# Where the LayerNorm and sum work between out-projection and FFN stands: order, rings and placement

## The chip, the cores and the metric

The kernel runs on one core of a Trainium2 chip. The metric is device time of one launch in microseconds. Three runs of the kernel before took 2832.81, 2822.79 and 2829.03 us, so the median is 2829.03 us.

## The reference

One layer of a streaming encoder over 17 chunks of 128 tokens (2048 new frames and 8 running streams of 16), all in float32, model width 1024, FFN width 4096:

```python
h = W_out [ gMLP heads (u * (W_s v + b)) || Mamba-2 SSD heads ] (x W_in)
x = LayerNorm(ALPHA * x + h)                      # "LN1", its result is called x1
x = LayerNorm(ALPHA * x + relu(x W1)^2 W2)        # "LN2", the output y
```

LayerNorm subtracts the mean over the 1024 features, multiplies by rsqrt(variance + 1e-5) and a gain, and adds a bias. ALPHA is 2^0.25.

## The kernel before, in words

The program has four stages: the mixer's heads, the out-projection with LN1, the first FFN product (FFN1) and the second (FFN2) with LN2. Matmuls are float32 in three passes: `split` rounds an operand to a high part (a cast on ACT, line 55) and leaves a low part (a subtraction on DVE, line 56), and the products hi·hi, hi·lo and lo·hi are summed in PSUM. So an operand is usable in full only after ACT and then DVE have touched it.

**Out-projection** (lines 617 to 712). The 17 chunks stand in 16 groups: the first is chunks 0 and 1, the last is 15 and 16, the rest one chunk each. A chunk takes 96 matmuls of 128x512 (16 slices of the 2048 mixed features, three passes, two halves of the output). The weights `wout` are held in eight tiles. Ahead of a group its mixed heads are loaded as `mxs` (gMLP part) and `mys` (SSD part, through a transpose to `myt`) into the shared ring `stage` (called `sp` in the functions) and split into `mx`. After a group, the chunk of x is loaded into `xr`, two scalar_tensor_tensor add the PSUM banks to it (line 708), `layer_norm` (lines 603 to 613) writes the result to another tile `x1`, and that is stored to DRAM.

**Sums for the FFN** (`Sums`, lines 728 to 790). FFN1 multiplies blocks of 2x2 with seven products in place of eight (Strassen's scheme in Winograd's form). It needs sums of token blocks of x1 and sums of w1 blocks. `x_piece(b, j)` loads two chunks of x1 (`xts`, four DMAs each), transposes them to `xtt` (line 43), makes four sums on DVE (lines 761 to 767) and stores seven parts to DRAM `xv`; `w1_piece` does the like for the weights (`w1p`). The pieces of token block 0 and the w1 sums are made during the out-projection (`during_out_proj`); those of blocks 1 and 2 are written in the FFN's steps g = 3, 6 and 9 of the block before. In the kernel before, the tiles `xts`, `xtt` and `xsum` all come from the ring `stage`.

**FFN1** (lines 793 to 910): 48 steps, 3 token blocks by 16 weight groups, each of seven products in the order 1, 6, 2, 7, 5, 4, 3. A product takes 12 matmuls of 128x384 (128x320 in block 2) from an x operand `xt` (from `xr`, loaded out of `xv`) and a weight operand `w` (from `w1l`, `w1r` or the sums `w1s`). The weights of a step are split during the step before, into a ring of ten tiles.

**FFN2** (lines 912 to 1080) makes seven products too, and `finish` does LN2 of a chunk. At the end of the program only `finish` of chunks 12 and 13 remains: statistics on DVE, rsqrt and the scaled mean `fnm` on POOL (lines 76, 77, 1000), the normalisation on ACT (line 1002), the gain and the bias on DVE (lines 1003, 1004), and the store.

**What sets the order.** The source gives the work in program order, and a scheduler with an estimate of the engines' times writes the order of each engine's queue ahead of the run; on the chip each engine takes its queue strictly in turn. What may go early is held back only by data and by the rings. All DMAs of these stages are issued by one queue, SP's, also strictly in turn: a DMA that waits for its data holds back all that stand behind it. An `x_piece` that is written in a late step, but whose x1 is long in DRAM and whose ring has room, can be put far ahead of that step.

## Time and profile before

| | us |
|---|---|
| median of three runs | 2829.03 |
| the profiled execution, its own time | 2822.72 |
| its span | 2821.0 |
| out-projection: first to last matmul | 1068.3 to 1467.9 |
| FFN1: first matmul to the stage's steady state | 1474.7 to about 1560 |
| FFN1 to its end | about 2159 |
| FFN2: last matmul | about 2807 |
| tail without matmuls | 2807 to 2821.0 |

TensorE (PE) is busy for 98% of the span, VectorE (DVE) for 64%, ScalarE (ACT) for 39% and GpSimd (POOL) for 14%. The mean granted clock is 0.99 of full speed. Idle time of PE is therefore rare and stands in a few places, which the profile's windows and PE's timeline show. In a timeline row, the bracket behind an instruction tells how long its engine had been idle before it and what released it. The rows that carry the argument are shown in the prediction.

### The profile page before, as it was taken

Reading aid. Unit: us, or ns where it says so; the run is one execution under the profiler, and the core shown is the slowest. Engines: PE = TensorE matmul, PEld = TensorE weight load, DVE = VectorE, ACT = ScalarE, POOL = GpSimd, SP = SyncE. Lnnn points to the kernel's source line nnn. Section 1 sums busy time; section 2 is a strip of 40 time slices with the busy share of each in tenths; the row PEclk is TensorE's granted clock in tenths of the full one; section 3 lists DMA queues with packets and bytes.
Section 4 is the critical chain, followed back from the end, with each engine's and each line's share of the span. In section 5 each row is a group of like instructions: output and inputs, shape, how many; then the busy total and the mean of one; then the engine's idle time right before and its main releaser. Section 6 shows DMA issues by size and latency. Waiting matters only on the chain.

```text
span 2821.0 us, 42133 instructions
## 1 busy us (share of the span) xinstructions
PE 2753.9 (98%) x15814; PEld 2525.6 (90%) x15814; DVE 1816.1 (64%) x2836; ACT 1096.0 (39%) x2024; POOL 395.1 (14%) x547
## 2 busy tenths in 40 slices
PE   9999999999999998999989999999999999999998
PEld 8988899999999997887879999999999888888886
DVE  6766667645585457665558667667775356644887
ACT  5445423323333333100115556556665323333343
POOL 2214223323233312000100000000000000000022
PEclk9999999999999999999999999999999999999999
DMA  9897888766697768888579858667877468855764
GB/s 316 257 297 250 281 288 272 228 221 217 218 305 220 244 218 302 279 260 273 159 217 342 292 214 286 222 223 259 276 233 259 152 233 300 299 173 190 272 206 171
DMA packets 492316, 699.83 MB, mean 248 GB/s; under 512 B 74560, under 2 KB 379088, under 8 KB 485584
## 3 DMA queue, kind: packets, MB, share of 16 engines
q1 hardware_dynamic: 492112, 697.14, 74.8%
q8 instruction: 124, 2.03, 0.3%
q14 instruction: 80, 0.66, 0.1%
HBM read 474.04 MB, written 223.00 MB: 247 GB/s over the span
## 4 chain that ended last, share of the span: by engine, by line
PE 77%; DMA 12%; DVE 6%; issue 1%; ACT 1%; POOL 1%; SPq 1%; DVEq 0%; ACTq 0%; POOLq 0%
PE pf L858 22%; PE pf L1075 22%; PE psfl L231 13%; PE pstl L239 10%; PE po L683 4%; PE yd L446 2%; DMA w1p<-in_w_ff 2%; DMA w1s<-w1p 2%; PE pf L1040 2%; DMA v<-v 1%; DMA xv<-xtt 1%; PE st L483 1%; DMA v<-vo 1%; DMA e<-at 1%; PE yo L489 1%
## 5 line engine op out<-in xcount | busy, mean ns | idle before, releaser
L858 PE MATMUL pf<-xt,w 128*128 128x384 f32 (+1 forms) x4032 | 671.8, 329 | 14.6 <-ACT w L55 11.4
L858 PEld LDWEIGHTS pf<-xt,w 128*128 128x128 f32 x4032 | 669.2, 189 | 17.4 <-ACT w L55 12.3
L1075 PE MATMUL pf<-w,ht 128*128 128x512 f32 x2688 | 618.2, 389 | 0.0
L1075 PEld LDWEIGHTS pf<-w,ht 128*128 128x128 f32 x2688 | 504.6, 188 | 104.6
L231 PE MATMUL psfl<-xw,w 128*128 128x384 f32 (+1 forms) x2880 | 494.9, 330 | 0.0
L231 PEld LDWEIGHTS psfl<-xw,w 128*128 128x128 f32 x2880 | 475.5, 188 | 9.0 <-issue 8.6
L239 PE MATMUL pstl<-w,xw 128*128 128x256 f32 (+1 forms) x3264 | 411.0, 286 | 8.4 <-ACT w L55 6.5
L239 PEld LDWEIGHTS pstl<-w,xw 128*128 128x128 f32 x3264 | 396.4, 190 | 21.0 <-issue 11.8
L683 PE MATMUL po<-wout,mx 128*128 128x512 f32 x1632 | 379.5, 394 | 12.0 <-ACT mx L55 8.1
L683 PEld LDWEIGHTS po<-wout,mx 128*128 128x128 f32 x1632 | 309.2, 190 | 79.1 <-ACT mx L55 8.8
L56 DVE TENSOR_TENSOR ht<-hr,ht 128x1536 fp32r<-128x1536 f32 (+1 forms) x84 | 132.3, 1577 | 128.0 <-ACT ht L55 126.5
L76 POOL TENSOR_SCALAR frs<-fmv 128x1 f32<-128x1 f32 x17 | 8.9, 524 | 1291.6 <-DVE fmv L996 1291.0
L55 ACT CAST ht<-hr 128x1536 fp32r<-128x1536 f32 (+1 forms) x84 | 112.2, 1337 | 194.7 <-PE pf L1075 142.0
L56 DVE TENSOR_TENSOR w<-w1s,w 128x512 fp32r<-128x512 f32 x192 | 132.0, 691 | 41.0 <-ACT w L55 36.0
L55 ACT CAST w<-w1s 128x512 fp32r<-128x512 f32 x192 | 118.3, 619 | 64.1 <-PE pf L858 57.0
L308 DVE SCALAR_TENSOR_TENSOR acc<-raw,cw,acc 128x640 f32<-128x640 f32 (+1 forms) x108 | 111.4, 1031 | 14.1 <-ACT acc L302 12.7
L56 DVE TENSOR_TENSOR w<-w2r,w 128x512 fp32r<-128x512 f32 x144 | 93.8, 686 | 36.8 <-ACT w L55 36.6
L55 ACT CAST w<-w2r 128x512 fp32r<-128x512 f32 x144 | 83.3, 618 | 87.3 <-PE pf L1075 56.9
L438 ACT ACTIVATE e<-e,nacum 128x128 f32<-128x128 f32 x272 | 83.6, 389 | 66.8 <-POOL e L69 66.7
L55 ACT CAST w<-w1r 128x512 fp32r<-128x512 f32 x96 | 59.4, 618 | 98.6 <-PE pf L858 95.3
L247 ACT ACTIVATE gt<-gt 128x256 f32<-128x256 f32 (+1 forms) x116 | 52.3, 451 | 95.9 <-DVE gt L246 95.9
L849 ACT ACTIVATE hc<-hc 128x384 f32<-128x384 f32 (+3 forms) x144 | 87.1, 608 | 1.8
(214 smaller groups left out, 2875.4 us busy)
## 6 DMA issues: line engine op xcount, KB each, us to landing
w1s<-w1s SPq DMA_DIRECT2D x48, 1024.0 KB, 6.7
hr<-hv SPq DMA_DIRECT2D x56, 768.0 KB, 6.1
w2r<-in_w_ff SPq DMA_DIRECT2D x112, 256.0 KB, 5.6
w<-w_x SPq DMA_DIRECT2D x12, 2048.0 KB, 10.5
w1r<-in_w_ff SPq DMA_DIRECT2D x48, 512.0 KB, 6.7
hv<-hs SPq DMA_DIRECT2D x32, 768.0 KB, 5.2
ws<-in_w_in SPq DMA_DIRECT2D x34, 512.0 KB, 7.7
e<-at SPq DMA_DIRECT2D x34, 512.0 KB, 6.7
```

The source lines that it names most:

```text
L55: nc.scalar.copy(hi, src)
L56: nc.vector.tensor_sub(lo, src, hi.bitcast(F32))
L231: nc.tensor.matmul(ps[:, :n], w[:, a, k, f * P:(f + 1) * P], xw[:, b, k, o:o + n], start=(q, i, k) == KORDER[0], stop=(q, i, k) == KORDER[-1])
L239: nc.tensor.matmul(ps[:, :n], xw[:, a, k, j * P:(j + 1) * P], w[:, b, k, :n], start=(q, i, k) == KORDER[0], stop=(q, i, k) == KORDER[-1])
L308: nc.vector.scalar_tensor_tensor(aa, raw[:, k:k + npr], cw[:, ft, k:k + 1], aa, op0=ALU.mult, op1=ALU.add)
L438: nc.scalar.activation(e[:, h], e[:, h], AF.Exp, bias=s["nacum"][:, i:i + 1])
L446: nc.tensor.matmul(yd[:, h * HD:(h + 1) * HD], e[:, h], xdt[:, h * HD:(h + 1) * HD], start=True, stop=True)
L683: nc.tensor.matmul(acc[c][d], m[c][k // 4][:, a, k % 4], W[q][:, w, i, d * 512:(d + 1) * 512], start=k == 0 and (a, w) == (0, 0), stop=k = ...
L849: nc.scalar.activation(t, t, AF.Square)
L858: nc.tensor.matmul(o, W[i][:, u, k], X[i][:, v, k, :n], start=q + k == 0 and not more, stop=q == 2 and k == 3, skip_group_check=True)
L1040: nc.tensor.matmul(ps[d], h[:, u, k, f], w[d][:, v], start=k + f + q == 0, stop=(k, f, q) == (n - 1, 1, 2))
L1075: nc.tensor.matmul(acc[l], h[:, u, m, j * P:(j + 1) * P], w[m][:, v], start=kg + q + m == 0, stop=(kg, q, m) == (3, 2, 3))
```

## The change

Five edits.

1. The tiles of `x_piece` come from a ring that the caller gives. During the out-projection it is a new ring `xp` of three tiles; in the FFN it is still `stage`, and a small copy on GpSimd from the current step's `c11` into the tile `xts` stands ahead of its loads, so that a piece written at step g cannot start before that step's product 2 is done.
2. LN1 of chunks 15 and 16 is not done in the out-projection. The residual sum is stored as `x0`, and `late_norm` loads it again at FFN1 steps (0, 11) and (0, 13), with the gain and the bias, normalises and stores x1.
3. LN1 works in place in `xr`; the second tile `x1` is gone.
4. In the FFN the ring `wr` (raw weights) is allocated first on the left side, and `x4` first on the right side ahead of `ho`, so that they lie over other tiles of the out-projection than before.
5. `finish` of chunks 12 and 13, the last two, normalises on DVE alone: four half-width scalar_tensor_tensor per chunk in place of one ACT and two DVE instructions, and a store for each half.

```diff
@@ mixer program
+    x0_d = {c: dr.tile([P, D], F32, name=f"x0_{c}") for c in range(NCH - LATE, NCH)}
...
-    out_proj(tc, right, psA, tail, A, dr, small, stage, rsqrt, split, yg_d, ys_d, x1_d, sums.during_out_proj)
-    ffn(tc, psA, A, O, dr, small, stage, rsqrt, split, x1_d, sums)
+    out_proj(tc, right, psA, tail, A, dr, small, stage, rsqrt, split, yg_d, ys_d, x0_d, x1_d, sums.during_out_proj)
+    ffn(tc, psA, A, O, dr, small, stage, rsqrt, split, x0_d, x1_d, sums)
@@ out_proj
             tp = rpool("to", 2)
+            xring = rpool("xp", 3)
...
-            o = tp.tile([P, D], F32, name="x1", tag="x1")
-            layer_norm(nc, small, rsqrt, o, x, g, b)
-            nc.sync.dma_start(x1_d[c], o)
-        done(n, ring)
+            if c < NCH - LATE:
+                layer_norm(nc, small, rsqrt, x, x, g, b)
+            nc.sync.dma_start(x1_d[c] if c < NCH - LATE else x0_d[c], x)
+        done(n, ring, xring)
@@ Sums
+LATE = 2
...
-    def tokens(self, c):
-        s = self.sp.tile([P, 4, 256], F32, name="xts", tag="st")
+    def tokens(self, c, ring, after):
+        s = ring.tile([P, 4, 256], F32, name="xts", tag="st")
+        if after is not None:
+
+            self.nc.gpsimd.tensor_copy(s[:, 0, :1], after)
         load_blocks(self.nc, s, self.x1_d[c])
-        t = self.sp.tile([P, KD, P], F32, name="xtt", tag="st")
+        t = ring.tile([P, KD, P], F32, name="xtt", tag="st")
         flip(self.nc, t, s)
         return t
...
-        s = self.sp.tile([P, 2, 4, P], F32, name="xsum", tag="st")[:, :, :, :m]
+        s = ring.tile([P, 2, 4, P], F32, name="xsum", tag="st")[:, :, :, :m]
...
-            self.x_piece(0, n // 2 - 2)
+            self.x_piece(0, n // 2 - 2, xring)
@@ ffn
+    wr = pool("wr", 3)
     rawp = pool("raw", 2)
     wp = pool("w4", 10)
     xp = pool("x3", 3)
-    wr = pool("wr", 3)
+    xp4 = pool("x4", 4, first, side="right")
     hop = pool("ho", 2, first, side="right")
-    xp4 = pool("x4", 4, first, side="right")
     sump = pool("ws", 2, first, side="right")
...
+    seen = [None]
...
             ahead(i)
+        seen[0] = c11[:, :1]
...
+    def late_norm(c):
+        t, g1, b1 = (sp.tile([P, D], F32, name=f"ln{i}", tag="st") for i in range(3))
+        nc.gpsimd.tensor_copy(t[:, :1], seen[0])
+        nc.sync.dma_start(t, x0_d[c])
+        nc.sync.dma_start(g1, A["ln1_g"].unsqueeze(0).to_broadcast([P, D]))
+        nc.sync.dma_start(b1, A["ln1_b"].unsqueeze(0).to_broadcast([P, D]))
+        layer_norm(nc, small, rsqrt, t, t, g1, b1)
+        nc.sync.dma_start(x1_d[c], t)
...
         if b < 2 and g in (3, 6, 9):
-            sums.x_piece(b + 1, g // 3 - 1)
+            sums.x_piece(b + 1, g // 3 - 1, sp, seen[0])
+        if b == 0 and g in (11, 13):
+            late_norm(NCH - LATE + (g - 11) // 2)
...
         rsqrt(rs, mv[:, 1:2], 1.0, EPS)
+        if c in THIRDS[2][0]:
+
+            o = sp.tile([P, D], F32, name="yo", tag="st")
+            halves = [slice(512 * d, 512 * d + 512) for d in range(2)]
+            for h in halves:
+                nc.vector.scalar_tensor_tensor(o[:, h], y[c][:, h], mv[:, 0:1], g2[:, h], op0=ALU.subtract, op1=ALU.mult)
+            for h in halves:
+                nc.vector.scalar_tensor_tensor(o[:, h], o[:, h], rs, b2[:, h], op0=ALU.mult, op1=ALU.add)
+                nc.sync.dma_start(O["y"][c][:, h], o[:, h])
+            return
         nm = small.tile([P, 1], F32, name="fnm")

```

How the engines' queues move, at three places. First, DVE where the first group of the out-projection (chunks 0 and 1) ends. `mx` from `mxs` is chunk 2's gMLP part, `po` are the first group's PSUM banks. Before:

```order
L777 TENSOR_TENSOR w1p_12433<-w1p_12432,w1p_12433 128x4x128
L778 TENSOR_TENSOR w1p_12432<-w1p_12432 128x4x128
L779 TENSOR_TENSOR w1p_12432<-w1p_12433,w1p_12432 128x4x128
L56 TENSOR_TENSOR mx_12075<-mxs_12073,mx_12075 128x512
L780 TENSOR_TENSOR w1p_12433<-w1p_12433,w1p_12432 128x4x128
L56 TENSOR_TENSOR mx_12078<-mxs_12073,mx_12078 128x512
L43 STREAM_TRANSPOSE myt_12086<-mys_12081 128x4x8x32
L56 TENSOR_TENSOR mx_12088<-myt_12086,mx_12088 128x512
L56 TENSOR_TENSOR mx_12091<-myt_12086,mx_12091 128x512
L708 SCALAR_TENSOR_TENSOR xr_12110<-xr_12110,po_11682 128x512
```

And in the changed kernel:

```order
L785 TENSOR_TENSOR w1p_12434<-w1p_12433,w1p_12434 128x4x128
L786 TENSOR_TENSOR w1p_12433<-w1p_12433 128x4x128
L711 SCALAR_TENSOR_TENSOR xr_12115<-xr_12115,po_11684 128x512
L711 SCALAR_TENSOR_TENSOR xr_12115<-xr_12115,po_11685 128x512
L787 TENSOR_TENSOR w1p_12433<-w1p_12434,w1p_12433 128x4x128
L609 BN_STATS lst_12121<-xr_12115 128x6
L711 SCALAR_TENSOR_TENSOR xr_12117<-xr_12117,po_11686 128x512
L609 BN_STATS lst_12121<-xr_12115 128x6
L711 SCALAR_TENSOR_TENSOR xr_12117<-xr_12117,po_11687 128x512
L788 TENSOR_TENSOR w1p_12434<-w1p_12434,w1p_12433 128x4x128
L609 BN_STATS lst_12134<-xr_12117 128x6
L56 TENSOR_TENSOR mx_12077<-mxs_12075,mx_12077 128x512
```

The four residual sums of chunks 0 and 1 and three of their statistics, which stood behind chunk 2's splits, now stand ahead of the first of them.

Second, SP's queue around the loads of FFN1's first step (`w1l`, `w1r`, `w1s` are its weights, `xr` from `xv0` its token sums, the others are stores of x1 sums and of LN1). Before, behind 40 DMAs on pieces of block 1 that stand between the store of chunk 13's x1 and this place:

```order
L819 DMA xr_14447<-xv0_11517 128x1536
L827 DMA w1l_14425<-in_w_ff1 128x4x128
L829 DMA w1r_14427<-in_w_ff1 128x1024
L819 DMA xr_14455<-xv0_11517 128x1536
L827 DMA w1l_14487<-in_w_ff1 128x4x128
L760 DMA xv1_11518<-xtt_15921 128x4x128
L763 DMA xv1_11518<-xsum_15923 128x4x128
L764 DMA xv1_11518<-xsum_15923 128x4x128
L766 DMA xv1_11518<-xtt_15921 128x4x128
L831 DMA w1s_14429<-w1s0_11520 128x2048
L831 DMA w1s_14491<-w1s1_11521 128x2048
L819 DMA xr_14463<-xv0_11517 128x1536
```

And in the changed kernel, where no DMA of block 1's pieces stands here any more:

```order
L706 DMA xr_14342<-in_x 128x1024
L836 DMA w1l_14394<-in_w_ff1 128x4x128
L838 DMA w1r_14396<-in_w_ff1 128x1024
L714 DMA x1_14_124<-xr_14131 128x1024
L836 DMA w1l_14456<-in_w_ff1 128x4x128
L706 DMA xr_14344<-in_x 128x1024
L828 DMA xr_14400<-xv0_11519 128x1536
L828 DMA xr_14408<-xv0_11519 128x1536
L838 DMA w1r_14458<-in_w_ff1 128x1024
L828 DMA xr_14416<-xv0_11519 128x1536
L714 DMA x0_15_127<-xr_14342 128x1024
L840 DMA w1s_14398<-w1s0_11522 128x2048
```

The first weights stand right behind the load of chunk 15's x, and `w1s` stands behind the store of `x0_15`.

Third, DVE at the end of the program. Before:

```order
L1024 TENSOR_TENSOR y15_21298<-y15_21298,pf_24766 128x512
L56 TENSOR_TENSOR w2_25365<-w2r_25363,w2_25365 128x512
L996 BN_AGGR fmv_25273<-st11_21331 128x2
L56 TENSOR_TENSOR w2_25368<-w2r_25363,w2_25368 128x512
L970 BN_STATS st14_21334<-y14_21297 128x6
L56 TENSOR_TENSOR w2_25379<-w2r_25377,w2_25379 128x512
L56 TENSOR_TENSOR w2_25382<-w2r_25377,w2_25382 128x512
L970 BN_STATS st15_21335<-y15_21298 128x6
```

And in the changed kernel:

```order
L56 TENSOR_TENSOR w2_25384<-w2r_25379,w2_25384 128x512
L991 BN_STATS st14_21350<-y14_21313 128x6
L56 TENSOR_TENSOR w2_25395<-w2r_25393,w2_25395 128x512
L56 TENSOR_TENSOR w2_25398<-w2r_25393,w2_25398 128x512
L991 BN_STATS st15_21351<-y15_21314 128x6
L56 TENSOR_TENSOR ht_25457<-hr_25455,ht_25457 128x1536
L1034 TENSOR_TENSOR yo_25244<-yo_25244,g2_21316 128x1024
L1017 BN_AGGR fmv_25320<-st14_21350 128x2
L1034 TENSOR_TENSOR yo_25270<-yo_25270,g2_21316 128x1024
```

The four full-width products and sums behind the ACT instruction have become eight half-width ones behind the statistics.

More of the change, by code (lines that the diff above doesn't have):

```diff
@@ L616, in out_proj @@
 @with_exitstack
-def out_proj(ctx, tc, right, ps, tail, A, dr, small, sp, rsqrt, split, yg_d, ys_d, x1_d, done):
+def out_proj(ctx, tc, right, ps, tail, A, dr, small, sp, rsqrt, split, yg_d, ys_d, x0_d, x1_d, done):
     nc = tc.nc
@@ L738, in __init__, with x_piece @@
         self.w1 = [dr.tile([P, 2, 1024], F32, name=f"w1s{g}") for g in range(NG)]
-    def tokens(self, c):
-        s = self.sp.tile([P, 4, 256], F32, name="xts", tag="st")
+    def tokens(self, c, ring, after):
+        s = ring.tile([P, 4, 256], F32, name="xts", tag="st")
+        if after is not None:
+            self.nc.gpsimd.tensor_copy(s[:, 0, :1], after)
         load_blocks(self.nc, s, self.x1_d[c])
-        t = self.sp.tile([P, KD, P], F32, name="xtt", tag="st")
+        t = ring.tile([P, KD, P], F32, name="xtt", tag="st")
         flip(self.nc, t, s)
         return t
-    def x_piece(self, b, j):
+    def x_piece(self, b, j, ring, after=None):
         nc = self.nc
         if j < len(THIRDS[b][0]):
-            l, r, m = self.tokens(THIRDS[b][0][j]), self.tokens(THIRDS[b][1][j]), P
+            l, r, m = *(self.tokens(THIRDS[b][i][j], ring, after) for i in range(2)), P
         else:
-            t = self.tokens(ODD)
+            t = self.tokens(ODD, ring, after)
             m = P // 2
@@ L782, in w1_piece, with during_out_proj @@
             nc.sync.dma_start(self.w1[g][:, k], w[k].rearrange("p k f n -> p (k f n)"))
-    def during_out_proj(self, n, ring):
+    def during_out_proj(self, n, ring, xring):
         for g in range(NG * n // 13, min(NG * (n + 1) // 13, NG)):
@@ L788, in during_out_proj, with ffn @@
         if n in (4, 6, 8):
-            self.x_piece(0, n // 2 - 2)
+            self.x_piece(0, n // 2 - 2, xring)
 @with_exitstack
-def ffn(ctx, tc, ps1, A, O, dr, small, sp, rsqrt, split, x1_d, sums):
+def ffn(ctx, tc, ps1, A, O, dr, small, sp, rsqrt, split, x0_d, x1_d, sums):
     nc = tc.nc
```

## The prediction

> **What bounds the kernel now.** I read the page's chain of waits first, then PE's timeline for its gaps, then windows around each gap, then the other engines' rows inside it.
>
> ```profile
> PE 77%; DMA 12%; DVE 6%; issue 1%; ACT 1%; POOL 1%; SPq 1%; DVEq 0%; ACTq 0%; POOLq 0%
> 1750.00:1820.00 70.00, 70.00 (x405) 70.00 (x404) 46.83 (x81) 38.61 (x70) 0.00 (x0) 1.00 0.65 233
> 2737.00:2807.00 70.00, 70.00 (x310) 57.71 (x308) 56.65 (x71) 29.58 (x37) 15.44 (x21) 1.00 0.61 214
> ```
>
> The columns of a window are its length, the busy time (and count) of PE, PEld, DVE, ACT and POOL, the granted clock, the DMA share and GB/s. PE leads the chain, and the two windows, in FFN1 and FFN2, have PE busy in all of their 70 us. There nothing but fewer matmuls could gain, and the change removes none; the first also gives FFN1's pace, 70/405 = 0.1728 us per matmul. What can be won stands in PE's gaps:
>
> ```profile
> 1101.13 7.49 PE L683 MATMUL po<-wout,mx 128*128 128x512 f32 x24 [0.37 <-ACT wout L636]
> 1115.64 3.02 PE L683 MATMUL po<-wout,mx 128*128 128x512 f32 x12 [1.55 <-DVE wout L637]
> 1124.94 203.43 PE L683 MATMUL po<-wout,mx 128*128 128x512 f32 x896 [1.55 <-DVE wout L637]
> ...
> 1334.50 133.39 PE L683 MATMUL po<-wout,mx 128*128 128x512 f32 x576 [6.13 <-ACT mx L55]
> 1474.66 4.71 PE L858 MATMUL pf<-xt,w 128*128 128x384 f32 x12 [6.76 <-ACT w L55]
> 1483.99 17.69 PE L858 MATMUL pf<-xt,w 128*128 128x384 f32 x84 [4.62 <-ACT w L55]
> 1503.87 56.43 PE L858 MATMUL pf<-xt,w 128*128 128x384 f32 x315 [2.19 <-ACT hc L861]
> ```
>
> Two gaps lie in reach of the change: 6.13 us at 1328 to 1334 in the out-projection, and the passage to FFN1, which idles 6.76 + 4.62 + 2.19 = 13.6 us. A gap costs more than itself, since the clock falls behind it:
>
> ```profile
> 1334.50 5.73 PE L683 MATMUL po<-wout,mx 128*128 128x512 f32 x13 [6.13 <-ACT mx L55]
> 1330.00:1340.00 10.00, 5.50 (x13) 4.34 (x14) 8.93 (x14) 2.28 (x4) 2.13 (x2) 0.66 0.87 267
> 1470.00:1480.00 10.00, 4.58 (x12) 3.56 (x12) 9.97 (x15) 3.46 (x3) 0.93 (x1) 0.65 1.07 368
> 1480.00:1490.00 10.00, 6.01 (x19) 6.01 (x20) 9.13 (x14) 5.74 (x9) 1.94 (x4) 0.50 1.03 377
> 1500.00:1510.00 10.00, 7.81 (x37) 7.49 (x36) 7.88 (x14) 4.76 (x9) 0.00 (x0) 0.83 1.07 343
> ```
>
> With a granted clock of 0.66, 13 matmuls took 5.73 us. The steady rate is (133.39 - 2.8)/576 = 0.2267 us, so 13 should take 2.95: 2.8 us lost.
>
> **The change, part by part.** The sum is made against the profiled execution, 2822.72 us, which is 6.3 below the median of the runs shown (2829.03). A difference under 0.3%, some 8.5 us, cannot be told from none here.
>
> *A: the passage (edits 1, 2, 4).* The rows inside it:
>
> ```profile
> 1459.54 3.68 SPq L37 DMA_DIRECT2D xts<-x  x8
> 1468.12 0.39 SPq L827 DMA_DIRECT2D w1l<-in_w_ff  x1
> ...
> 1472.62 1.47 ACT L55 CAST xt<-xr 128x1536 fp32r<-128x1536 f32 x1 [14.08 <-DMA xr<-xv]
> ...
> 1476.76 1.09 SPq L831 DMA_DIRECT2D w1s<-w1s  x2
> 1480.06 4.60 SPq L37 DMA_DIRECT2D xts<-x  x4
> 1483.32 0.62 ACT L55 CAST w<-w1s 128x512 fp32r<-128x512 f32 x1 [5.10 <-DMA w1s<-w1s]
> ```
>
> From the last out-projection matmul (1334.50 + 133.39 = 1467.9) to the end of the third PE row (1560.3), 411 matmuls take 92.4 us. At the pace above they need 71.0, so 21.4 are lost: 13.6 idle, the rest a slow clock. The cause is SP's order: loads and stores of block 1's and 2's pieces (`xts`, `xv`) stand ahead of `w1l` (issued 1468.12) and `w1s` (1476.76), whose cast could begin only at 1483.32. Edit 1 takes these pieces away from here, and edits 2 and 4 take the LN1 work and let the weights' ring lie over tiles that fall free early. I place what is left of the waits from the order. Product 1's x and weights are then ready before the last out-projection matmul, so its 12 matmuls (2.1 us) start at once. Product 6 needs `w1s`, which stands behind the store of `x0_15`. That store waits for chunk 15's residual sum, about 1.6 us before the last matmul, so `w1s` is issued 0.7 before it; 6.5 us from issue to cast, as in the rows above (1476.76 to 1483.32), puts the wait at 5.8 - 2.1 = 3.7 us. Products 6 and 2 then run to about 10 us. Product 7's x is the last of 3.25 MB in the queue (two `w1s` of 1 MB, the 0.75 MB of x, the store of `x0_16`): 9.3 us at the 368 GB/s of the window 1470 to 1480, so it lands near 8.6 at the earliest, and its cast of 1.47 stands on ACT behind weight casts of 0.62 each: done between 11.6 and 13, a wait of up to 3 us, and 1 more for its low part on DVE. That is 8 us, and 0 to 2.5 of slow clock: I take 9.5 lost, so a **gain of 11.9**. Bounds: no wait left but the 3.7 gives a gain of 17.7; that wait, a second one as long as the 6.76 of before, and 4 of slow clock (14.5) a gain of 7.
>
> *B: the stall at 1328 (edit 1).*
>
> ```profile
> 1324.77 0.73 SPq L768 DMA_DIRECT2D xv<-xtt  x1
> 1330.06 0.33 SPq L648 DMA_DIRECT2D mxs<-yg  x1
> ...
> 1333.83 1.14 ACT L55 CAST mx<-mxs 128x512 fp32r<-128x512 f32 x2 [37.39 <-DMA mxs<-yg]
> ```
>
> Chunk 11's `mxs` is loaded at 1330.06, after SP stood from 1325.5 behind the stores of an x piece in the shared ring; ACT waited 37 us for it. With a ring of its own for the pieces, `mxs` no longer waits for `xtt` and `xsum` to fall free, and groups last 96 x 0.2267 = 21.8 us against 3.8 from issue to cast. **Gain 6.1 + 2.8 = 8.9**; it is 0 if `mxs` is held by other tiles of that ring.
>
> *C: the end of the first group (edits 1 and 3).* Here the order of DVE changes for the worse.
>
> ```profile
> 1124.91 0.33 SPq L648 DMA_DIRECT2D mxs<-yg  x1
> ...
> 1130.49 1.15 ACT L55 CAST mx<-mxs 128x512 fp32r<-128x512 f32 x2 [2.75 <-DMA mxs<-yg]
> ...
> 1131.14 0.69 DVE L56 TENSOR_TENSOR mx<-mxs,mx 128x512 fp32r<-128x512 f32 x1
> ...
> 1131.80 0.90 SPq L703 DMA_DIRECT2D xr<-in_x  x2
> ...
> 1138.67 1.29 DVE L708 SCALAR_TENSOR_TENSOR xr<-xr,po 128x512 f32<-128x512 f32 x2 [2.42 <-DMA xr<-in_x]
> ```
> ```profile
> L607 DVE BATCH_NORM_STATS2 lst<-xr 128x6 f32<-128x512 f32 x34 | 22.6, 684 | 0.0
> L708 DVE SCALAR_TENSOR_TENSOR xr<-xr,po 128x512 f32<-128x512 f32 x34 | 21.8, 682 | 15.4 <-PE po L683 13.0 <-DMA xr<-in_x 2.4
> L777 DVE TENSOR_TENSOR w1p<-w1p 128x512 f32<-128x512 f32 x15 | 10.4, 692 | 57.5 <-DMA w1p<-in_w_ff 52.7 <-issue 4.8
> L43 DVE STREAM_TRANSPOSE xtt<-xts 128x1024 f32<-128x1024 f32 x16 | 19.9, 1241 | 19.4 <-DMA xts<-x 15.4 <-DMA xv<-xtt 3.9
> L612 DVE SCALAR_TENSOR_TENSOR x<-xr,lmv,g 128x1024 f32<-128x1024 f32 x17 | 21.8, 1282 | 0.4
> ```
>
> The first group ends at 1124.94 + 203.43 - 9 x 21.8 = 1132.2 (nine chunks follow up to the stall). Before, chunk 2's first low part was begun at 1131.14, in time. Now seven instructions that wait for the first group's own matmuls and for `xr`, with two or three `w1p` sums between, stand ahead of it on DVE, and two loads of `xr` (1 MB) stand ahead of `mxs` on SP. By the 368 GB/s above that 1 MB takes 2.8 us. So the first half's cast, over at 1131.1 before (half of 1.15), is over at 1133.9: 1.7 us idle, since the group ends at 1132.2. `xr` takes 1138.67 - 1131.80 = 6.9 us at most, so DVE can begin near 1131.2; four sums, three statistics, two `w1p` sums and the split, each 0.64 to 0.69, end at 1137.6. Chunk 2's fifth matmul, due at 1134.8, needs that: 2.8 us idle. With 0 to 2 of slow clock, **a cost of 5.5**. Bounds: 2, if `xr` lands early and DVE keeps up; 9, if `xr` needs its 6.9 from a later issue.
>
> *D: the last LayerNorm (edit 5).*
>
> ```profile
> 2808.92 0.40 DVE L996 BATCH_NORM_AGGREGATE fmv<-st 128x2 f32<-128x12 f32 x2
> ...
> 2811.16 2.37 ACT L1002 ACTIVATE yo<-y,fnm,frs 128x1024 f32<-128x1024 f32 x2 [7.69 <-POOL fnm L1000]
> 2812.43 2.36 DVE L1003 TENSOR_TENSOR yo<-yo,g 128x1024 f32<-128x1024 f32 x2 [3.12 <-ACT yo L1002]
> 2814.71 2.36 DVE L1004 TENSOR_TENSOR yo<-yo,b 128x1024 f32<-128x1024 f32 x2
> ```
>
> Before, DVE stood from 2809.3 to 2812.4 for POOL and ACT, and ended at 2817.07. Now eight half-width instructions of 0.64 (half of line 612's 1.28; line 708's, with PSUM, take 0.682) follow 2809.4 at once: 2814.5. **Gain 2.6**, and no more than 0.5 beside it for half as large a last store. Bounds 1.5 and 3.5.
>
> *E: pieces and late norms in FFN1.*
>
> ```profile
> x<-x SPq DMA_DIRECT2D x17, 512.0 KB, 7.7
> ```
>
> Each of six pieces costs DVE two transposes of 1.25 and four sums of 0.69, 5.3 us; each late norm two statistics and two normalisations of line 612's length (1.28), 4 us. In all 40 us, in a stage where DVE stands idle for 70 - 46.83 of each 70 us and the weights are split up to a step ahead. I cost them at nothing; without that cover the price is about 4 us each. Edit 3 puts the load of `xr` on SP behind the landing of a store; hidden too, as the store is issued a group (21.8 us) ahead of that load's use and takes 7.7 us to land.
>
> **Sum:** -11.9 - 8.9 + 5.5 - 2.6 = -17.9: 2804.8 for the execution profiled, and 2829.0 - 17.9 = 2811 against the median. I take 2810.
>
> The slow clock is the least sure item. In these rows it follows idle times of 4.6 us and more (0.50 to 0.66), and also the 3.3 us ahead of the row at 1101.13, whose 24 matmuls took 7.49 us against 5.44; after 1.55 us at 1115.64 there is almost nothing, 3.02 against 2.72. The Trainium skill, page "TensorE: Matmul & The Clock Gate", section "Why this matters for your kernels", says to leave "No PE-idle gaps >~3µs between matmul bursts", and "What's actually happening" has half clock after an idle window of about 3.4 us until about 3.4 us of sustained work. That speaks against this change: by it each of my new waits of 3 to 4 us would cost up to half of 3.4 more, an estimate of 1.7 each, and the sum would be some 3 us smaller, -15. The rows agree that short waits can be punished, the one at 1101.13 by 2 us.
>
> **The rivals.** (1) *Waits vanish wholly*: the passage loses only 1.4, and C is hidden since `xr` lands early. -20 - 8.9 - 2.6 = -31.5: 2797. For it: most loads now stand a group ahead. Against it: `w1s` behind the store.
> (2) *The wait re-forms on the loads*: `x0` stores, `xr` and `w1s` share SP's queue, the passage gains 5 only, C costs 9. -5 - 8.9 + 9 - 2.6 = -7.5: 2821.5. For it: the queue is strict, and DMA shares of 1.03 to 1.07 above.
> (3) *Slower*: in FFN1 DVE and SP stand behind a piece's loads in turn, since they are now tied to their step; while DVE waits for `xts` no weight is split, and PE runs dry. Price: 4.62 idle, as at the passage, and 1 of clock, at six pieces, 34 us: 2811 + 34 = 2845. It decides once DVE's delay exceeds the lead of the ring of ten tiles, about 20 us (1.4 steps of 84 x 0.1728 = 14.5). Against it: a delay of 5.3 + 4 is half of that.
> (4) *The passage does not clear*, as something other than the pieces held SP: -6: 2823.
>
> **How the numbers follow.** Chances: forecast 0.47, (1) 0.18, (2) 0.19, (3) 0.10, (4) 0.06. Faster by over 0.3% means below 2820.5: nearly all of the forecast, all of (1), two fifths of (2), a third of (4), together 0.74. Slower than 2837.5 is (3) alone, most of it: 0.08. The rest, 0.18, is the same. The forecast's own range, from the bounds of A and C, is 2801 to 2819. The range of 8 in 10 reaches to (1) and (2): 2797 to 2828.
>
> **What would show it.** In the changed profile: no `xts` or `xv` on SP between 1440 and 1500, the gap behind the last 128x512 matmul broken into one of 3 to 4 us released by ACT's cast of `w` (from `w1s`) and one on `xt`; no gap near 1330; a new gap of 3 to 6 us near 1133, released by `mx` (line 56); PE full in every 70 us window from 1560 to 2150; a tail of some 11 us behind the last matmul. FFN1 windows with PE under 70 would prove rival 3, a gap of over 6 us at the passage rival 2 or 4.

## The result and the profile after

The changed kernel took 2813.47 us (median of 18 runs, 2803.84 to 2818.81) against 2826.44 us for the kernel before (18 runs): a ratio of 0.995, 95% interval 0.9939 to 0.9961, 13.0 us faster by the medians. The forecast was 2810, in a range of 2797 to 2828. The two profiled executions lie closer together, 2822.72 and 2814.9 us (spans 2821.0 and 2813.2). In the ratios further down, one execution of experiment 11's kernel, which took 8760.61 us, is left out.

First PE's timeline of the changed kernel; the columns are start, length, engine, line, operation, tiles, count, and in the bracket the idle time ahead and its releaser. (Line 685 is the out-projection, 867 FFN1.)

```profile
1128.95 7.57 PE L685 MATMUL po<-wout,mx 128*128 128x512 f32 x32 [1.55 <-DVE wout L639]
1138.58 1.19 PE L685 MATMUL po<-wout,mx 128*128 128x512 f32 x4 [2.06 <-ACT mx L55]
1141.54 186.56 PE L685 MATMUL po<-wout,mx 128*128 128x512 f32 x816 [1.77 <-DVE mx L56]
...
1329.12 11.17 PE L685 MATMUL po<-wout,mx 128*128 128x512 f32 x48 [1.02 <-DVE mx L56]
1341.07 11.20 PE L685 MATMUL po<-wout,mx 128*128 128x512 f32 x48 [0.77 <-DVE mx L56]
1354.69 120.71 PE L685 MATMUL po<-wout,mx 128*128 128x512 f32 x524 [2.43 <-DVE mx L56]
1475.23 2.27 PE L867 MATMUL pf<-xt,w 128*128 128x384 f32 x12
1481.15 6.01 PE L867 MATMUL pf<-xt,w 128*128 128x384 f32 x24 [3.64 <-ACT w L55]
1487.37 0.97 PE L867 MATMUL pf<-xt,w 128*128 128x384 f32 x4 [0.21 <-ACT xt L55]
...
1489.42 67.08 PE L867 MATMUL pf<-xt,w 128*128 128x384 f32 x385 [1.09 <-DVE xt L56]
1557.91 42.32 PE L867 MATMUL pf<-xt,w 128*128 128x384 f32 x242 [1.41 <-DVE hc L878]
```

The 6.13 us at 1328 and the 6.76 + 4.62 + 2.19 us of the passage are gone. In their place stand eight short waits in the out-projection and at the passage, and one of 1.41 us in FFN1. Windows over two of them (PE's busy time and count come first behind the length, the granted clock third from the end):

```profile
1140.00:1150.00 10.00, 8.46 (x31) 6.89 (x32) 9.95 (x14) 1.14 (x2) 3.66 (x4) 0.83 1.01 293
1350.00:1360.00 10.00, 7.57 (x26) 5.75 (x26) 6.56 (x10) 1.14 (x2) 0.00 (x0) 0.83 0.70 196
```

The granted clock is 0.83 in each. By stages, from PE's timelines: from the last head matmul of the mixer (`sg`) to the last of the out-projection (or to FFN1's first, where that starts sooner) 346.6 us before and 349.9 after; from there to FFN2's first matmul 684.4 and 672.5; from the last matmul to the end 13.9 and 10.6. So the stretch to FFN2, with the passage in it, gave 11.9, the tail gave 3.3, and the out-projection took 3.3 more in these two executions. The tail's new rows on DVE, where ACT's normalisation and the two products behind it stood:

```profile
2804.75 2.73 DVE L1025 SCALAR_TENSOR_TENSOR yo<-y,fmv,g 128x512 f32<-128x512 f32 x4
...
2807.39 2.73 DVE L1027 SCALAR_TENSOR_TENSOR yo<-yo,frs,b 128x512 f32<-128x512 f32 x4
```

### The profile page after: what moved, and what is told of

Same layout as the page of the kernel before. It is cut to its first block, busy times and chain, and to the rows that moved or that the text cites. A ratio compares the mean times of both kernels' runs of the same rounds, so it can differ in the third digit from the quotient of the medians.

```text
span 2813.2 us, 42173 instructions
## 1 busy us (share of the span) xinstructions
PE 2752.9 (98%) x15814; PEld 2521.6 (90%) x15814; DVE 1807.9 (64%) x2840; ACT 1090.5 (39%) x2022; POOL 402.6 (14%) x558
## 4 chain that ended last, share of the span: by engine, by line
PE 76%; DMA 13%; DVE 6%; issue 2%; POOL 1%; ACT 1%; SPq 1%; DVEq 0%; ACTq 0%; POOLq 0%
PE pf L867 22%; PE pf L1106 22%; PE psfl L233 12%; PE pstl L241 9%; PE po L685 5%; DMA w1p<-in_w_ff 2%; PE yd L448 2%; DMA e<-at 2%; PE pf L1071 2%; DMA v<-vo 1%; DMA xts<-x 1%; DMA w1s<-w1p 1%; PE st L485 1%; PE sg L539 1%; PE yo L491 1%
## 5 line engine op out<-in xcount | busy, mean ns | idle before, releaser
L685 PE MATMUL po<-wout,mx 128*128 128x512 f32 x1632 | 379.2, 393 | 12.8 <-DVE mx L56 6.4
L858 ACT ACTIVATE hc<-hc 128x384 f32<-128x384 f32 (+2 forms) x144 | 87.1, 607 | 1.6
```

What stands on the lines that cost most here:

```text
L685: nc.tensor.matmul(acc[c][d], m[c][k // 4][:, a, k % 4], W[q][:, w, i, d * 512:(d + 1) * 512], start=k == 0 and (a, w) == (0, 0), stop=k = ...
L858: nc.scalar.activation(t, t, AF.Square)
```

## The experiments

Each kernel was timed beside the kernel before on the same chip; ratios are to it, with the 95% interval. The changed kernel, 1 to 4, 5 to 8 and 9 to 12 were timed in four sets, with medians of before from 2826.44 to 2829.92 us, so kernels of different sets are compared by their ratios. The stage times are those of one profiled execution each, in the same three stretches as above:

| kernel | ratio | out-projection | to FFN2 | tail |
|---|---|---|---|---|
| before | 1 | 346.6 | 684.4 | 13.9 |
| changed | 0.9950 (0.9939 to 0.9961) | 349.9 | 672.5 | 10.6 |
| 1 pin alone | 0.9967 (0.9953 to 0.9981) | 350.9 | 678.3 | 14.0 |
| 2 ring and in place | 1.0026 (1.0014 to 1.0038) | 350.2 | 690.4 | 13.9 |
| 3 in place alone | 1.0031 (1.0020 to 1.0043) | 358.0 | 682.8 | 14.0 |
| 4 tail alone | 0.9987 (0.9971 to 1.0002) | 352.1 | 683.4 | 10.6 |
| 5 first group mended | 0.9940 (0.9924 to 0.9956) | 339.8 | 672.0 | 10.6 |
| 6 w1 sums on GpSimd | 0.9961 (0.9945 to 0.9976) | 347.2 | 676.4 | 10.5 |
| 7 x0 stores off SP | 0.9957 (0.9942 to 0.9973) | 344.8 | 675.6 | 10.8 |
| 8 all three | 0.9954 (0.9939 to 0.9969) | 349.0 | 675.6 | 10.8 |
| 9 no late norms | 0.9992 (0.9978 to 1.0006) | 349.6 | 683.0 | 10.6 |
| 10 old ring places | 0.9947 (0.9928 to 0.9966) | 348.3 | 674.9 | 10.6 |
| 11 pieces doubled | 1.0039 (1.0020 to 1.0058) | 349.9 | 706.1 | 10.8 |
| 12 best | 0.9928 (0.9907 to 0.9949) | 344.1 | 677.3 | 10.8 |

The first stretch of one and the same order varies by some 5 us between executions (346.6 and 352.1 in the kernels before and 4, whose out-projection is the same), so it is read by its gaps.

**1. The pin alone**, on the kernel before:

```diff
+        if after is not None:
+            self.nc.gpsimd.tensor_copy(s[:, 0, :1], after)
...
-            sums.x_piece(b + 1, g // 3 - 1)
+            sums.x_piece(b + 1, g // 3 - 1, seen[0])
```

> The kernel before, and only the second half of edit 1: the x1 pieces of the FFN are tied to their step by the GpSimd copy, and nothing else is changed. My theory (the pieces put ahead on SP cost the passage its 21.4 us): the loss between the last 128x512 matmul and 1560 falls from 21 to some 8 to 12 us, and the whole kernel gains 9 to 13 us, nearly all that the full change gained. Rival (the passage needs the late norms and the reordered rings as well, since the load of w1l and the store of x1_15 hold SP): the loss stays above 15 us, gain under 6. The stall of 6 us near 1330 stays by both.

By the ratio it gains 9.3 us (2817.71 against 2829.7), inside what my theory gave. The profile lies between the theory and the rival: the first 425 matmuls of FFN1 take 86.8 us, where 73.4 are due, so 13.4 of the 21.4 us lost remain at the passage, and to FFN2 it saves 6.1 us of the full change's 11.9. So the pieces on SP were one cause, and not the only one. The stall in the out-projection stayed, 0.72 + 8.53 us.

**2. Ring and in-place LN1**, on the kernel before. The rows changed are those of the change in `out_proj`, `tokens` and `x_piece`, without `after` and without LATE.

```diff
+            xring = rpool("xp", 3)
...
-            o = tp.tile([P, D], F32, name="x1", tag="x1")
-            layer_norm(nc, small, rsqrt, o, x, g, b)
-            nc.sync.dma_start(x1_d[c], o)
-        done(n, ring)
+            layer_norm(nc, small, rsqrt, x, x, g, b)
+            nc.sync.dma_start(x1_d[c], x)
+        done(n, ring, xring)
```

> The kernel before with the ring of three tiles for the x1 pieces of the out-projection; LN1 is done in place, since the ring has no room beside the second tile. The pieces of blocks 1 and 2 are not tied to their steps. My theory: no wait on mxs near 1330; in its place several waits of 1 to 2.5 us on mx, as in the changed kernel's profile, because DVE then stands behind the loads of w1p: out-projection 3 us shorter there, 4 to 5 us longer behind the first group; passage unchanged (21 us lost). In all -1 to +4 us. Rival (the shared ring was the whole cause): the stall goes without a successor, -9 +5 = -4 us, and the waits of the changed kernel at 1328 to 1357 come from another edit.

Slower by 7.4 us (0.0026 of 2829.7), more than either theory gave, for a reason that none named: the stretch to FFN2 grew by 6 us to 690.4. Its waits at the passage are 8.06 + 4.95 + 0.81 + 3.90 us, against 6.76 + 4.62 + 2.19 before; the last is on an x operand whose load was issued right behind two loads of `xts` and took 12.8 us to land. Experiment 3, the same edit without the ring, has 682.8, so the ring costs this while the pieces are not tied. In the out-projection it went as my theory had it: 1.60 + 2.21 us behind the first group, then waits on `mx` of 0.97 and 1.97 us in the place of the stall.

**3. In place alone**, on the kernel before: the last hunk of experiment 2 without the rings.

> The kernel before with edit 3 alone: LN1 in place in xr, no second tile. My theory: this edit is what puts the first group's residual sums ahead of chunk 2's splits on DVE, so a new gap of 3.5 to 5 us stands behind the first group (released by mx, in two pieces), with 1 to 1.5 us of slow clock: 4 to 6 us slower than before. Rival (the gap comes from elsewhere, or is made up later since the stall near 1330 shrinks by as much): no difference, within 2 us.

Slower by 8.8 us (0.0031 of the same time), more than the 4 to 6 expected.

```profile
1144.36 1.19 PE L683 MATMUL po<-wout,mx 128*128 128x512 f32 x4 [1.02 <-ACT mx L55]
1148.36 154.41 PE L683 MATMUL po<-wout,mx 128*128 128x512 f32 x668 [2.81 <-DVE mx L56]
1307.58 45.43 PE L683 MATMUL po<-wout,mx 128*128 128x512 f32 x192 [4.80 <-ACT mx L55]
1356.60 133.55 PE L683 MATMUL po<-wout,mx 128*128 128x512 f32 x576 [3.59 <-ACT mx L55]
```

The gap behind the first group is there with this edit alone: 1.02 + 2.81 = 3.83 us, the same 3.83 as in the changed kernel. So this edit alone is enough for term C. And the waits on `mxs` (released by ACT) stay without the piece's own ring, 4.80 + 3.59 us, while experiment 2, with the ring, has 2.94 us of another kind. So the ring does remove the stall.

**4. The tail alone**, on the kernel before: the new branch of `finish`.

```diff
+        if c in THIRDS[2][0]:
+            ...
+            return
         nm = small.tile([P, 1], F32, name="fnm")
```

> The kernel before with edit 5 alone: the shorter last LayerNorm of chunks 12 and 13. My theory: the stretch from the last matmul to the end falls from 13.9 to about 10.6 to 11.3 us, a gain of 2.6 to 3.3 us, everything else alike. Rival (the end is set by the landing of the stores, which move the same bytes): under 1 us.

The tail fell from 13.9 to 10.6 us, 3.3 as my theory had it; the ratio's 3.7 us is not clear of nothing. Its out-projection, the same as before's, shows the stall again, larger, 1.94 + 8.91 us; the second of the two:

```profile
1351.05 133.15 PE L683 MATMUL po<-wout,mx 128*128 128x512 f32 x576 [8.91 <-ACT mx L55]
```

**5. The first group mended**, on the changed kernel: xr's load is tied behind chunk 2's split.

```diff
             xs[c] = tp.tile([P, D], F32, name="xr", tag="xr")
+            if n == 0:
+                nc.gpsimd.tensor_copy(xs[c][:, :1], m[2][0][:, 1, 3, :1].bitcast(F32))
             nc.sync.dma_start(xs[c], A["x"][c])
```

> The changed kernel, with the first group's loads of xr tied (by a GpSimd copy of one column) behind chunk 2's second low part, so that its residual sums can stand only behind chunk 2's splits on DVE, as they did before. My theory: the gap of 2.06 + 1.77 us behind the first group goes, with the 1.4 us of slow clock: 4 to 5.5 us faster than the changed kernel. Rival (mxs lands late in any case, since the out-projection's weights still load): 2 us or less.

2809.25 us. By the ratios that is 0.0010, some 3 us, below the changed kernel, less than the 4 to 5.5 expected, and the two intervals overlap. In the profile the gap is gone:

```profile
1133.06 231.75 PE L685 MATMUL po<-wout,mx 128*128 128x512 f32 x1020 [1.55 <-DVE wout L639]
```

From 1133.06 on PE runs through the group's end without a wait, and the stretch is 10 us shorter than the changed kernel's. The gap and its slow clock were 5.7 of that; for the rest, only one wait, of 1.85 us, is left of the later three.

**6. The sums of the w1 pieces on GpSimd**, on the changed kernel:

```diff
-        nc.vector.tensor_add(a22, a21, a22)
+        nc.gpsimd.tensor_add(a22, a21, a22)
...
```

> The changed kernel with the four sums of a w1 piece on GpSimd in place of DVE. In the changed kernel DVE waits 6 to 8 us at a time for w1p to land, with chunk splits queued behind it; that is my cause for the waits of 1.02, 0.77 and 2.43 us on mx between 1328 and 1357. My theory: these three go (and their slow clock, 1.8 us), 4 to 6 us faster than the changed kernel, though a sum on GpSimd takes longer than DVE's 0.69. Rival (the waits come from the DMA queue, which these sums do not touch): the waits stay, or come back on mxs, under 2 us of difference.

No gain: 2815.87. In the out-projection PE now waits 1.97, 2.59 and 4.41 us for `mx`. The rows ahead of the last of these:

```profile
1375.89 1.29 POOL L785 TENSOR_TENSOR w1p<-w1p 128x512 f32<-128x512 f32 x1 [10.72 <-DMA w1p<-in_w_ff]
...
1382.07 1.28 DVE L615 SCALAR_TENSOR_TENSOR xr<-xr,lrs,b 128x1024 f32<-128x1024 f32 x1 [19.42 <-POOL lrs L77]
1383.28 0.68 DVE L56 TENSOR_TENSOR mx<-myt,mx 128x512 fp32r<-128x512 f32 x1
```

GpSimd waits 10.72 us for `w1p`, LN1's rsqrt stands behind that sum on GpSimd, the second half of the norm waits 19.42 us for it on DVE, and the split of `mx` stands behind the norm. The late load now reaches PE over one engine more. The gap behind the first group did go in this kernel, as its order there changed too.

**7. The x0 stores off SP**, on the changed kernel:

```diff
-            nc.sync.dma_start(x1_d[c] if c < NCH - LATE else x0_d[c], x)
+            (nc.sync if c < NCH - LATE else nc.gpsimd).dma_start(x1_d[c] if c < NCH - LATE else x0_d[c], x)
```

> The changed kernel with the two x0 stores issued by GpSimd's queue, so that on SP the load of w1s no longer stands behind a store that waits for the last group's residual sum. My theory: w1s is issued several us sooner and the wait of 3.64 us on w behind product 1 goes, with its 1.9 us of slow clock; the wait of 1.3 on xt may grow to 2 to 3 instead: 3 to 5 us faster than the changed kernel. Rival (the tiles for w1s come free only at the end of the out-projection anyway): no difference.

```profile
1137.75 328.69 PE L685 MATMUL po<-wout,mx 128*128 128x512 f32 x1436 [2.60 <-DVE mx L56]
...
1468.58 0.48 ACT L870 COPY hc<-pf 128x384 f32<-128x384 f32 x1 [4.69 <-PE pf L867]
...
1469.63 4.43 PE L867 MATMUL pf<-xt,w 128*128 128x384 f32 x24 [1.09 <-ACT w L55]
...
1476.00 1.47 ACT L55 CAST xt<-xr 128x1536 fp32r<-128x1536 f32 x1
...
1477.52 0.97 PE L867 MATMUL pf<-xt,w 128*128 128x384 f32 x4 [3.46 <-ACT xt L55]
1479.31 113.75 PE L867 MATMUL pf<-xt,w 128*128 128x384 f32 x637 [0.82 <-DVE xt L56]
```

The wait on `w1s` shrank to 1.09 us, and product 7's x made up for it, 3.46 + 0.82 us. I put this down to 2 MB of `w1s` ahead of that x on SP, but ACT's rows show another limit: from its copy at 1468.58, which waits for product 1, to the cast of that x at 1476.00 ACT is never idle, with twelve casts of weights in between. The x had landed 1.1 us before its cast. The 1.09 us that stays is ACT's too, the copy of 0.48 us and the first cast of 0.62. Both theories missed: the tiles were free (the first `w1s` was issued 5.4 us ahead of the last out-projection matmul), but nothing was gained. The first row is of interest for the out-projection, which this edit leaves alone: 1436 matmuls with no gap. The waits of 1.02, 0.77 and 2.43 us of the changed kernel do not come in each execution.

**8. All three**: 2814.73 us.

> The three mends in one kernel: first group's xr loads tied, w1 sums on GpSimd, x0 stores off SP. If the three waits are independent, the gains add: 10 to 16 us faster than the changed kernel, near 2800 us. If they share a cause (DMA queue), the sum falls well short of that: under 6.

The gains did not add. With the sums on GpSimd, the waits in the out-projection are 1.25, 2.10 and 5.98 us, and the passage has 1.09 and 3.46 us, as in 6 and 7.

**9. No late norms**, on the changed kernel:

```diff
-LATE = 2
+LATE = 0
```

> The changed kernel without edit 2: LN1 of chunks 15 and 16 stays in the out-projection (in place), nothing is put off to the FFN. My theory, after the run with the pin alone gave only about half of the passage's gain: the late norms carry a part of it, since DVE's and SP's work for the two norms stands between the loads of the first step. So the stretch from the last out-projection matmul to FFN2 grows by 2 to 4 us against the changed kernel (672.5 us). Rival (DVE and SP have room once the pieces are gone): within 1 us, and edit 2 was worth nothing.

I had this much too small. The stretch to FFN2 grew by 10.5 us, and of the kernel's gain nothing is left that is clear of noise (0.9992).

```profile
1491.85 1.27 DVE L615 SCALAR_TENSOR_TENSOR xr<-xr,lrs,b 128x1024 f32<-128x1024 f32 x1
1493.15 0.33 SPq L714 DMA_DIRECT2D x<-xr  x1
...
1496.96 1.47 ACT L55 CAST xt<-xr 128x1536 fp32r<-128x1536 f32 x1 [10.02 <-DMA x<-xr]
...
1498.48 1.97 PE L867 MATMUL pf<-xt,w 128*128 128x384 f32 x5 [10.53 <-ACT xt L55]
```

ACT's cast of an x operand waits 10.02 us, and what releases it is the landing of the store of chunk 16's x1. That store could be issued only behind the norm's last instruction on DVE (line 615). So I take it that `xt` lies over the tile that this store reads, and PE waits 10.53 us for a tile, not for a load. In the changed kernel the store is that of `x0_16`, which needs no norm: it was issued 1.3 us behind the last out-projection matmul, here 17.9 us. These are the ring places of edit 4; no run takes the late norms away with the old places.

**10. Old ring places**, on the changed kernel: the three rows of edit 4 put back.

> The changed kernel with edit 4 undone: the rings wr, x4 and ho stand where they stood before. My theory: the ring wr then lies over tiles of the out-projection that fall free late, so w1l and the first weights come after the last matmul, and product 1 waits some 4 to 7 us as it did before (6.76): 4 to 8 us longer from the last out-projection matmul to FFN2. Rival (the loads are late only because of the pieces on SP): within 1 us.

No difference in time (2813.92, a ratio of 0.9947 against 0.9950). The first `w1l` is issued only 7.2 us ahead of the last out-projection matmul, in the changed kernel 38.1 us, yet it lands in time and product 1 starts without a wait. The first 425 matmuls of FFN1 take 80.5 us (81.3 in the changed kernel); the stretch to FFN2 is 2.4 us longer because of gaps later, behind the pieces. At the passage the rival holds: edit 4 brought nothing that these runs can show.

**11. Pieces doubled**, on the changed kernel. Each piece is made twice, with the same values.

```diff
             sums.x_piece(b + 1, g // 3 - 1, sp, seen[0])
+            sums.x_piece(b + 1, g // 3 - 1, sp, seen[0])
```

> The changed kernel with each of the six x1 pieces of the FFN made twice, one right behind the other, with the same values: 5.3 us more of DVE, 8 more loads and 7 more stores at each. The changed kernel has gaps of 1.41 and 0.51 us behind the pieces. My theory (term E, hidden by the lead of the split weights): 0 to 1.5 us more per piece, FFN1 up to 6 us longer. Rival 3 (the lead is used up, DVE's waits come through): 4 us or more for each piece, FFN1 20 us longer or more.

33.6 us more to FFN2, 5.6 for each added piece: rival 3's price. A group row of FFN1 (count, then busy time and mean, then idle time ahead and its releasers), and one gap:

```profile
L867 PE MATMUL pf<-xt,w 128*128 128x384 f32 x2576 | 459.8, 340 | 23.9 <-DVE hc L878 11.5 <-ACT hc L870 6.7 <-ACT xt L55 5.7
L43 DVE STREAM_TRANSPOSE xtt<-xts 128x1024 f32<-128x1024 f32 x22 | 27.4, 1246 | 69.6 <-DMA xts<-x 60.2 <-DMA hv<-hc 7.8 <-DMA hv<-hs 1.7
```
```profile
1650.70 1.25 DVE L43 STREAM_TRANSPOSE xtt<-xts 128x1024 f32<-128x1024 f32 x1 [3.78 <-DMA hv<-hc]
1651.87 0.52 DVE L878 TENSOR_TENSOR hc<-hc,pf 128x384 f32<-128x384 f32 x1
...
1652.44 15.19 PE L867 MATMUL pf<-xt,w 128*128 128x384 f32 x86 [1.54 <-DVE hc L878]
```

Of PE's 23.9 us of gaps 18.2 are released by DVE's and ACT's work on `hc`, that is by the emptying of PSUM banks, 5.7 by the cast of an x operand, and none by a split of weights. DVE stood 60.2 us behind loads of `xts` in all.

**12. The best**: the mends of 5 and 7, and `w1s` of steps 1 and 2 tied behind the split of x:

```diff
+        if after is not None:
+            nc.gpsimd.tensor_copy(s[:, 0, 0, 0, :1], after)
...
-            raw = load_w1(*steps[k + 1])
+            raw = load_w1(*steps[k + 1], X[(7, 5)[k]][:, 0, 0, :1].bitcast(F32) if k < 2 else None)
```

> The changed kernel with the first group's xr loads tied behind chunk 2's splits (as in the run that mended the first group), the x0 stores issued by GpSimd, and the sums w1s of FFN1's steps 1 and 2 tied behind the split of product 7's and product 5's x, so that on SP the x of product 7 stands ahead of them. With the x0 stores off SP alone, the wait of 3.64 us on w fell to 1.09 but one of 3.46 us on product 7's x took its place. My theory (2 MB of w1s ahead of that x made it late): both waits stay under 1.5 us, slow clock under 1, passage 3 to 5 us shorter than in the run that only mended the first group, about 2804 to 2806 us. Rival (any order leaves the same bytes to load, and the wait moves on once more, to step 1's weights): no gain over that run.

```profile
1471.59 5.48 PE L871 MATMUL pf<-xt,w 128*128 128x384 f32 x28 [1.09 <-ACT w L55]
1478.06 5.97 PE L871 MATMUL pf<-xt,w 128*128 128x384 f32 x32 [0.99 <-DVE xt L56]
1486.10 14.09 PE L871 MATMUL pf<-xt,w 128*128 128x384 f32 x79 [2.07 <-ACT w L55]
```

The waits on `w1s` and on product 7's x are 1.09 and 0.99 us now, but step 1's `w` comes late, 2.07 us: the rival's "moves on once more". The first 425 matmuls of FFN1 take 79.5 us, 1.6 less than in experiment 5, where 3 to 5 were expected, and the whole stretch to FFN2 is 5.3 us longer than there, with gaps of up to 2.06 us behind the pieces. At 2808.37 us it is the lowest median of all, and not to be told from experiment 5's 2809.25. By the ratios the two lie 6 and 3 us below the changed kernel, with overlapping intervals.

## Why the prediction was right, point by point

**A, the passage: right in size, its cause in part.** Forecast 11.9 gained, measured 13.6 at the passage itself (21.4 less the 7.8 below). The rows of the changed kernel follow the working closely:

```profile
1473.80 0.32 SPq L714 DMA_DIRECT2D x<-xr  x1
1474.17 1.57 SPq L840 DMA_DIRECT2D w1s<-w1s  x2
...
1480.47 0.62 ACT L55 CAST w<-w1s 128x512 fp32r<-128x512 f32 x1 [2.45 <-DMA w1s<-w1s]
...
1485.83 1.49 ACT L55 CAST xt<-xr 128x1536 fp32r<-128x1536 f32 x1
...
1487.62 1.75 DVE L56 TENSOR_TENSOR xt<-xr,xt 128x1536 fp32r<-128x1536 f32 x1
```

The store of `x0_15` is followed by `w1s` at 1474.17, its cast comes 6.3 us later (6.5 forecast), and PE waits 3.64 us (3.7 forecast). The wait on product 7's x is 0.21 + 1.09 us in place of 3 + 1, and slow clock cost 1.9 us (24 matmuls in 6.01 us against 4.15). In all 425 matmuls took 81.3 us from 1475.23 against 73.4, 7.8 us lost where I had 9.5. What the working left open is which edit does it. I named the pieces as "the cause". Experiment 1 gives them 8.0 of the 13.6 at the passage. Experiment 9 shows that without the late norms nearly nothing is gained (683.0), by a wait for a tile that the prediction does not name. Edit 4, which I counted in, adds nothing at the passage (experiment 10). On the stretch to FFN2, each on its own base, the ring and LN1 in place cost 6.0 (experiment 2), the tie saves 6.1 (1) and the late norms 10.5 (9), in all 10.6 of the 11.9. The late norms may thus in part make good what other edits cost: experiment 1, which leaves both norms where they were and lacks the ring and edits 2 to 4, loses only 5.6 us more at the passage than the changed kernel.

**B, the stall at 1328: the step that was mis-sized.** The prediction took the whole 8.9 as gained. The wait on `mxs` is gone, and the ring is what removes it (experiments 2 and 3). But DVE became next in line, which I had looked for behind the first group only, though in the profile before DVE waits 6.18 us for `w1p` at this very place and is then at work without a break up to the split of `mx` at 1334.48 (first row; the others are the changed kernel's):

```profile
1329.38 0.69 DVE L777 TENSOR_TENSOR w1p<-w1p 128x512 f32<-128x512 f32 x1 [6.18 <-DMA w1p<-in_w_ff]
...
1324.06 0.69 DVE L785 TENSOR_TENSOR w1p<-w1p 128x512 f32<-128x512 f32 x1 [6.18 <-DMA w1p<-in_w_ff]
...
1328.39 0.68 DVE L56 TENSOR_TENSOR mx<-myt,mx 128x512 fp32r<-128x512 f32 x1
...
1339.72 0.69 DVE L785 TENSOR_TENSOR w1p<-w1p 128x512 f32<-128x512 f32 x1 [8.16 <-DMA w1p<-in_w_ff]
1340.33 0.68 DVE L56 TENSOR_TENSOR mx<-mxs,mx 128x512 fp32r<-128x512 f32 x1
...
1353.34 0.69 DVE L785 TENSOR_TENSOR w1p<-w1p 128x512 f32<-128x512 f32 x1 [3.71 <-DMA w1p<-in_w_ff]
1353.95 0.69 DVE L56 TENSOR_TENSOR mx<-myt,mx 128x512 fp32r<-128x512 f32 x1
```

DVE waits 6.18, 8.16 and 3.71 us for `w1p`, and the split of `mx` stands behind, the first time with five other instructions between, then directly. That cost 1.02 + 0.77 + 2.43 us of idle time and 2.5 of slow clock (48, 48 and 25 matmuls in 11.17, 11.20 and 7.60 us, where 10.88, 10.88 and 5.67 are due): 6.7 of the 8.9 were given back in this execution, a gain of 2.2. Over executions the term is larger: the three profiles with before's order there have 6.13, 0.72 + 8.53 and 1.94 + 8.91 us of waits, the six with the changed order (the changed kernel, 2, 7, 9, 10 and 11) 4.22, 2.94, 0, 2.74, 2.08 and 2.91. The means are 8.7 and 2.5, so a gain of some 6 us of idle time. No run loads `w1p` sooner, so that this load is the cause is read from the order of the queues and not tested.

**C, the first group: right.** Forecast 5.5 in two waits of 1.7 and 2.8; measured 2.06 + 1.77, and 1.9 of slow clock (4 and 31 matmuls in 1.19 and 8.63 us, due 0.91 and 7.03): 5.7. The cast of `mx` waited for `mxs` behind `xr` on SP, and its low part came last on DVE, as the order had it:

```profile
1127.76 0.80 SPq L706 DMA_DIRECT2D xr<-in_x  x2
1128.92 0.33 SPq L650 DMA_DIRECT2D mxs<-yg  x1
...
1137.91 1.14 ACT L55 CAST mx<-mxs 128x512 fp32r<-128x512 f32 x2 [5.93 <-DMA mxs<-yg]
...
1140.81 0.68 DVE L56 TENSOR_TENSOR mx<-mxs,mx 128x512 fp32r<-128x512 f32 x1
```

**D, the tail: right.** 3.3 against 2.6. DVE's part is 2.5 (from 10.0 to 7.5 us behind the last matmul); the time from DVE's end to the end of the program fell by another 0.8, where I had 0.5 at most for the smaller last store.

**E, FFN1: small but not nothing, with the wrong point of decision.** Costed at nothing, measured 1.41 + 0.51 us in gaps:

```profile
1553.90 1.25 DVE L43 STREAM_TRANSPOSE xtt<-xts 128x1024 f32<-128x1024 f32 x1 [3.36 <-DMA xts<-x]
...
1557.31 0.55 DVE L878 TENSOR_TENSOR hc<-hc,pf 128x384 f32<-128x384 f32 x1
```

DVE waits 3.36 us for `xts` with the sum that empties a PSUM bank (line 878) queued behind, and PE waits for that bank. From the 421st to the 2601st matmul of FFN1, which at 0.1728 us need 376.7 us, the kernel before took 379.1 and the changed kernel 381.6; over all profiles it is 378.9 to 380.3 where the pieces are not tied (before, 2, 3 and 4) and 380.4 to 387.5 in the nine kernels with tied single pieces, means of 379.3 and 382.9. So the term costs some 2.5 us in the two profiles and 3.5 in the mean. Rival 3 was to decide once some 20 us of split weights were used up. It decides earlier and by another path: the gap of 1.41 us comes with 3.36 us of waiting and at most 5.3 of work on DVE, a second copy in experiment 11 costs 5.6 us each, and the waits are on banks. I had no good reason to call the term nothing.

**The rivals.** Rival 1's passage was not reached (7.8 lost, not 1.4). Rival 2's wait on `w1s` came, but at the forecast's price. Rival 3 needs twice the pieces. Rival 4 falls with the passage.

**The slow clock.** Forecast 0 to 2.5 at the passage, measured 1.9. These losses hold up to 0.2 us that a row shows behind no wait too (12 matmuls in 2.27 us, 2.07 due). The rule of the Trainium skill, page "TensorE: Matmul & The Clock Gate", section "What's actually happening", would by my estimate cost 1.7 us behind a wait of 3 to 4 us, and this trace agrees: 1.9 behind 3.64. The limit of about 3 us in that page's section "Why this matters for your kernels" does not hold in the out-projection, where a wait of 2.43 us cost 1.9 too (25 matmuls in 7.60).

**The signs and the sum.** Of the signs named, "no gap near 1330" failed; the others came, with PE busy for 69.5 to 70.0 us of each 70 us window from 1560 to 2120. In time, -17.9 was forecast and -13.0 measured over the medians. That 2813.47 lies within 3.5 us of the 2810 forecast is in part luck, since the forecast started from 2829.03, the median of three runs of the kernel before, and eighteen give 2826.44. In the two profiles B gave 6.7 less than forecast, E cost 1.9 and C 0.2 more, A gave 1.7 and D 0.7 more, which leaves -11.5, and the three stretches add up to -11.9. The profiles themselves differ by 7.8, as the mixer's last head matmul came 4.0 us later in the changed kernel's (1125.3 against 1121.3), ahead of everything that the change moves.

## What to carry to other kernels

When a wait is taken away, read what stands next to it on the engine that fed it: here, by the order of the queues, one late load (`w1p`) reached PE over DVE once `mxs` was in time, and over GpSimd and DVE once its sums were moved. A move of work is worth what stood behind it, not what it takes itself: two LayerNorms of 4 us on DVE were worth 10.5 us at the passage, as the cast of an x operand waited for the store of their result. And a cover is measured by doubling what it hides: the pieces in FFN1 looked free at 70 - 46.83 us of idle DVE, and the second copy cost its full price, 5.6 us against 5.3 of work.

## What the runs showed of the hardware

Short waits were dearer than I had them. One of 2.43 us was followed by 25 matmuls in 7.60 us (5.67 due), one of 2.06 and one of 1.77 with 1.2 us of work between by 31 in 8.63 (7.03 due), while waits of 0.77 and 1.02 us cost 0.3, which is hardly more than matmuls show behind no wait at all (12 in 2.27, 2.07 due). And the same order of instructions gave the mixer's last head matmul at 1121.3 us in one execution and at 1132.1 in another (before and experiment 4): single profiles of this kernel compare only by stretches and gaps.
